# A two-layer block with routed experts on one Trainium2 core: empty slots left out of the row gather, and the gate matrix's last tile split like the others

## The chip, the cores and the metric

The program runs on one core of one Trainium2 chip. The metric is the device time of one execution in microseconds (us), lower is better. A core has four compute engines (TensorE or PE for matmuls, VectorE or DVE, ScalarE or ACT, GpSimd or POOL), an engine SyncE (SP) whose queue issues most of the DMAs, and 16 DMA engines that move data between the chip's memory (HBM) and the core's own memory. Each engine runs its instructions in order and waits for the others by semaphores.

## What is computed

The reference runs two blocks one after the other on 512 tokens of width 1024, each two layers deep. The first block is sparse attention beside a gated recurrence. The second block mixes (a short convolution in layer 0, a gated linear recurrence in layer 1), then sends each token through two of 32 experts. The part that the change touches is that expert step, which runs once in each layer of the second block:

```python
def hier_moe(x, w_rg, b_rg, w_re, b_re, w_gate, w_up, w_down):
    ...
    _, g_top = lax.top_k(pg, 1)             # one of 4 groups per token
    ...
    top_p, top_i = lax.top_k(pe, TOP_K)     # two of its 8 experts
    expert = g_top * EXPERTS_PER_GROUP + top_i
    weight = pg_top * top_p
    ...
    def expert_block(args):
        idx, e = args
        xb = x_pad[idx]                     # rows of the tokens sent to expert e
        hb = jax.nn.silu(xb @ w_gate[e]) * (xb @ w_up[e])
        return hb @ w_down[e]
    ...
    y = jnp.zeros((n + 1, d), x.dtype).at[tok_pad].add(contrib)
```

`w_gate` and `w_up` are 1024x512 per expert, `w_down` is 512x1024, all float32. 512 tokens times two choices make 1024 token-expert pairs per layer.

## The kernel before

**Precision by splitting.** A float32 weight tile is split into a high and a low part: ACT writes the high part (`wh`, line 425) and DVE the rest (`wl = w - wh`, line 426), both in a type that TensorE takes in one pass. The token rows are split alike. The 128 columns that TensorE holds still are 64 slots' high parts beside the same 64 slots' low parts, so two matmuls, one with `wh` and one with `wl`, give all four products. Both tensors come from rings: four tiles `wh`, four `wl`, and four tiles `X` that hold a high and a low part together (lines name `X<-w` and `X<-w,X`).

**Slots.** `route` (line 1336) ranks the tokens of each expert and fills 64 slots per expert. A matmul against one-hot rows gives, per slot and expert, one more than the number of the token-expert pair that sits there, or 0 for an empty slot. `tokens` (line 1483) makes the token number `tk` from it: less 1, not below 0, halved. An empty slot so names token 0. `slots` (line 1489) makes `mp`, the row to which the slot's result goes: less 1, plus 2^20 for an empty slot, which lies past the table's end. `rows` (line 1496) writes the normalised tokens to a table `xr` in HBM.

**Gather and scatter.** `gather` (line 1517) takes the rows of two experts (128 slots) from `xr` with one indirect DMA on POOL's queue (line 1522) into a tile `xg` from a ring of two, and then has PE transpose them, and ACT and DVE split them into `pk`, with the float32 copy of the last k-tile in `xf`. `finish` (line 1616) writes the 64 result rows of one expert with another indirect DMA (line 1624) to `ym` at the rows `mp`. Both are issued with a bound (`bounds_check`) beyond which a row is dropped without an error.

**The stream.** `experts` (line 1727) lists units of work. A weight tile `w` is 1 MB (128 partitions x 2048 float32), six per expert: two of gate (k = 0, 1), two of up (k = 2, 3), two of down (k = 4, 5), from a ring of six. SP issues their loads (line 1561), each once its buffer has been read. Each tile has two halves of 1024 columns, `part` 0 and 1; a half is one unit, except that k = 5 has one unit only. `cut` (line 1565) splits a unit's half into `wh`/`wl` or into `X`, and TensorE's matmuls for it come AHEAD = 6 units later in the program.

**The part left unsplit.** For three 512-column tiles per expert only the first 512 columns of the last half are split, and the other 512 (`also`) are multiplied in float32 with the unsplit rows:

```python
m = 1 if k in (1, 3) and part else 2
also = w[:, 3] if m == 1 else w[:, 2:4] if k == 5 else None
h, l = self.cut(w[:, 2 * part:2 * part + m], n // 4 % 2)
```

These are the last tile of gate (k = 1), of up (k = 3), and the last of down (k = 5). The float32 matmul stands at line 1583 (gate and up) and line 1612 (down). It reads the tile `w` itself, so that tile's buffer comes free only behind it.

**The order.** `pin` (line 1627) fixes each compute engine's order to the order in which the program lists its work. Per expert DVE's list has: the `wl` or `X` of eleven units, two adds for `yb` (line 1623) of the expert before, two multiplications for `mth` (lines 1597 and 1598), and the split `hk` (line 426) of the hidden rows. ACT has the high parts of the same, the copies of accumulators (lines 1765 and 1622), a tanh (line 1596), and `hk` (line 425), which needs `mth`. In every second expert, two `pk` splits and `xf` (line 1538) come in. TensorE's accumulators are three tiles `acc`; a new expert's first matmul waits until ACT has copied the up product out (line 1765).

A loop for experts with more than 64 tokens (line 1661) stands ahead of the stream; it runs zero times on this data. Its block `overflow` uses the same functions.

Of the kernel before, what the change touches and what calls it, by code (L numbers as in the profile page):

```python
# [13 lines left out]
I32 = mybir.dt.int32  # L14
# [3 lines left out]
OP = mybir.AluOpType  # L18
AX = mybir.AxisListType

P = 128
# [158 lines left out]
class Net:  # L180
# [1155 lines left out]
    def route(self, i):  # L1336
# [81 lines left out]
        for k in range(2):  # L1418
# [3 lines left out]
            for c in range(NC):  # L1422
                pe.matmul(mps, R[:, c].rearrange("p b s -> p (b s)"), idk[:, k, c], start=(k + c == 0),
                          stop=(k == 1 and c == NC - 1))
        tk = self.t([P, N_EXP // 2], "tk", 1, I32)
        tk2 = self.t([P, N_EXP], "tk2", 1, I32)
        self.tokens(tk2, mps)
        for b in range(2):
            v.tensor_copy(tk[b * BLK:(b + 1) * BLK], tk2[b * BLK:(b + 1) * BLK, b::2])
        mp = self.t([BLK, N_EXP], "mp", 1, I32)  # L1430
        self.slots(mp, mps[:BLK])

# [24 lines left out]
        def further():  # L1457
# [22 lines left out]
            return place, more  # L1480
        return table, tk, mp, further, weights

    def tokens(self, tk, ps):

        v = self.nc.vector
        v.tensor_scalar(tk, ps, -1.0, 0.0, op0=OP.add, op1=OP.max)
        v.tensor_scalar(tk, tk, 1, None, op0=OP.logical_shift_right)

    def slots(self, mp, ps):

        v = self.nc.vector
        em = self.t([BLK, N_EXP], "em", 1)[:, :ps.shape[1]]
        v.tensor_scalar(em, ps, 0.0, float(1 << 20), op0=OP.is_equal, op1=OP.mult)
        v.scalar_tensor_tensor(mp, ps, -1.0, em, op0=OP.add, op1=OP.add)
# [21 lines left out]

    def gather(self, table, idx, m):

        nc = self.nc
        v, act, pe = nc.vector, nc.scalar, nc.tensor  # L1520
        xg = self.t([P, D], "xg", 2)
        nc.gpsimd.indirect_dma_start(out=xg[:m], out_offset=None, in_=table[:, :],  # L1522
# [52 lines left out]

    def inner(self, ps, x, k, h, l, also):

        pe = self.nc.tensor
        pk, xf = x
        for q in range(h.shape[1]):  # L1580
            pe.matmul(ps, pk[:, k + q], h[:, q], start=(k + q == 0), stop=False)  # L1581
            if also is not None:
                pe.matmul(ps[0:BLK], xf, also, start=False, stop=False, skip_group_check=True)  # L1583
            pe.matmul(ps, pk[:, k + q], l[:, q], start=False, stop=also is not None)  # L1584

# [57 lines left out]
    def moe(self, i, xs, nxt):  # L1643
# [4 lines left out]
        table, tk, mp, further, weights = self.route(i)  # L1648
        pair = lambda q: self.gather(table, tk[:, q:q + 1], P)
        g = pair(0)  # L1650
# [10 lines left out]
        with self.tc.For_i(0, extra, 1) as b:  # L1661
# [14 lines left out]
            self.slots(mc, mps)  # L1676
            self.tokens(tc, mps)
            go = self.gather(table, tc, BLK)
            next(go)
# [20 lines left out]
    def overflow(self, i, e, x, mp, ym):  # L1700
# [3 lines left out]
        for up in range(2):  # L1704
            ps = self.acc()
            for k in range(0, KT, 2):
                w = self.weights(i, e, 2 * up + k // 4, k // 2 % 2)
                m = 1 if k == KT - 2 else 2
                h, l = self.cut(w[:, 0:m])
                self.inner(ps, x, k, h[:, :m], l[:, :m], w[:, 1] if m == 1 else None)  # L1710
            gu.append(room())
            self.nc.scalar.activation(gu[up], ps, AF.Copy)
# [14 lines left out]
    def experts(self, i, ws, xs2, pair, mp, ym, weights):  # L1727
# [14 lines left out]
        for n in range(len(units) + AHEAD):  # L1742
            if n < len(units):
                e, k, part = units[n]
                if part == 0 and (e, k) not in ws:
                    ws[e, k] = self.weights(i, e, k)
                w = ws[e, k]
                m = 1 if k in (1, 3) and part else 2
                also = w[:, 3] if m == 1 else w[:, 2:4] if k == 5 else None
                h, l = self.cut(w[:, 2 * part:2 * part + m], n // 4 % 2)  # L1750
                ready.append((h[:, :m], l[:, :m], also))
            self.pin()
# [205 lines left out]
```

## Time and profile before

| what | value |
|---|---|
| three timed runs | median 3081.84 us (3077.51 to 3083.08) |
| the profiled execution | 3084.05 us, of which the span of its instructions is 3082.3 us |
| busy share of the span | PE 93%, DVE 80%, ACT 57%, POOL 15% |
| mean granted TensorE clock | 0.975 of full speed |
| HBM traffic | 573.60 MB read, 31.49 MB written |

The profile is one execution of the same program. A busy share is an average over stages of different kinds; the two expert streams lie at about 1590 to 2130 us and 2445 to 2985 us of the span, and there the DMA engines are busy nearly all the time, elsewhere a fifth to a third.

### The profile page before, as it was taken

What the parts mean: (1) busy time and instruction counts of PE and PEld (TensorE: products, weight loads), DVE (VectorE), ACT (ScalarE), POOL (GpSimd) and SP (SyncE); (2) the same over time, 40 slices, a digit from 0 to 9 for tenths busy, and PEclk for the clock granted to TensorE, in tenths of its full rate; (3) what the DMA queues carried; (4) which work ended last, traced back from release to release, by engine and by line L of the source; (5) the groups of instructions that cost most, each with busy time, mean ns of one, the idle gap of its engine ahead of it and who ended that gap; (6) DMA issues with size and microseconds to landing.
All of it is one profiled execution on the core that took longest, in us unless ns stands there. A gap on an engine that the chain in (4) does not pass through costs nothing.

```text
span 3082.3 us, 39081 instructions
## 1 busy us (share of the span) xinstructions
PE 2881.6 (93%) x13517; PEld 2160.2 (70%) x13517; DVE 2464.3 (80%) x4540; ACT 1756.1 (57%) x2953; POOL 472.8 (15%) x457
## 2 busy tenths in 40 slices
PE   7998999999999999999979999998998799999987
PEld 6677778886787778878856666665776566666656
DVE  7899787867999578855558888887789588888876
ACT  3454343544454433542357877776476577777874
POOL 1111110011121010120011121111122111121112
PEclk9999999999999999999989999999999899999998
DMA  5211122242222222241259999997123399999981
GB/s 156 82 62 62 62 77 69 83 128 94 74 62 61 77 69 79 86 130 62 95 216 396 406 404 401 407 399 277 65 86 110 151 385 405 404 408 408 406 313 59
DMA packets 248663, 599.29 MB, mean 194 GB/s; under 512 B 29212, under 2 KB 159726, under 8 KB 215694
## 3 DMA queue, kind: packets, MB, share of 16 engines
q1 hardware_dynamic: 237582, 567.38, 49.1%
q0 software_dynamic: 10880, 29.37, 2.7%
q8 instruction: 108, 1.77, 0.2%
q14 instruction: 93, 0.76, 0.1%
HBM read 573.60 MB, written 31.49 MB: 196 GB/s over the span
## 4 chain that ended last, share of the span: by engine, by line
PE 38%; issue 33%; DVE 18%; POOL 7%; ACT 3%; DMA 2%; POOLq 0%; SPq 0%; ACTq 0%; DVEq 0%
PE acc L522 9%; PE acc L521 9%; PE acc L520 9%; POOL ym L1624 4%; DVE wl L426 3%; DVE tmp L953 2%; PE aux L432 1%; POOL xg L1522 1%; PE aux L463 1%; PE aux L843 1%; DMA xg<-xr,tk 1%; PE aux L1111 1%; PE aux L1106 1%; DVE r L1082 1%; DVE r L1081 1%
## 5 line engine op out<-in xcount | busy, mean ns | idle before, releaser
L425 ACT ACTIVATE wh<-w 128x1024 fp32r<-128x1024 f32 (+1 forms) x592 | 577.8, 1003 | 370.2 <-PE acc L521 323.0
L426 DVE TENSOR_TENSOR wl<-w,wh 128x1024 fp32r<-128x1024 f32 (+1 forms) x592 | 674.1, 1164 | 71.1 <-ACT wh L425 66.7
L520 PE MATMUL acc<-X,wh 128*128 128x512 f32 (+1 forms) x1504 | 606.3, 403 | 18.5 <-DVE tmp L898 6.4
L521 PE MATMUL acc<-X,wh 128*128 128x512 f32 (+1 forms) x1536 | 615.8, 401 | 0.6 <-DVE X L426 0.6
L522 PE MATMUL acc<-X,wl 128*128 128x512 f32 (+1 forms) x1504 | 601.9, 401 | 4.9 <-DVE wl L426 4.9
L426 DVE TENSOR_TENSOR X<-w,X 128x1024 fp32r<-128x1024 f32 (+1 forms) x352 | 380.9, 1122 | 64.0 <-ACT X L425 63.2
L425 ACT ACTIVATE X<-w 128x1024 fp32r<-128x1024 f32 (+1 forms) x352 | 326.7, 971 | 34.3 <-DMA w<-in_w_exp_gate_dram 10.1
L520 PEld LDWEIGHTS acc<-X,wh 128*128 128x128 f32 (+1 forms) x1504 | 285.3, 190 | 82.1 <-DVE tmp L898 7.3
L521 PEld LDWEIGHTS acc<-X,wh 128*128 128x128 f32 (+1 forms) x1536 | 291.3, 190 | 59.4 <-DVE X L426 1.2
L522 PEld LDWEIGHTS acc<-X,wl 128*128 128x128 f32 (+1 forms) x1504 | 284.8, 189 | 64.9 <-DVE wl L426 7.1
L1624 POOL DMA_INDIRECT ym<-yb,mp x64 | 136.0, 2125 | 811.9 <-DVE yb L1623 811.9
L1581 PE MATMUL acc<-X,pk 128*128 128x512 f32 x448 | 185.6, 414 | 18.2 <-ACT tmp L1765 12.6
L1581 PE MATMUL acc<-wh,pk 128*128 128x512 f32 x448 | 181.9, 406 | 15.5 <-ACT tmp L1765 15.5
L1584 PE MATMUL acc<-X,pk 128*128 128x512 f32 x448 | 185.9, 415 | 0.0
L1584 PE MATMUL acc<-wl,pk 128*128 128x512 f32 x448 | 183.5, 410 | 0.0
L1583 PE MATMUL acc<-w,xf 128*64 128x512 f32 x256 | 137.3, 618 | 0.0
L1584 PEld LDWEIGHTS acc<-X,pk 128*128 128x128 f32 x448 | 86.3, 193 | 66.0 <-DVE X L426 18.7
L1593 PEld LDWEIGHTS aux<-fold,tmp 128*128 128x128 f32 x1024 | 126.1, 194 | 8.8 <-ACT tmp L1765 3.5
L1584 PEld LDWEIGHTS acc<-wl,pk 128*128 128x128 f32 x448 | 84.5, 189 | 65.8 <-issue 16.2
L479 POOL TENSOR_TENSOR tmp<-tmp,tmp 128x512 f32<-128x512 f32 x60 | 86.4, 1444 | 280.9 <-ACT tmp L472 234.5
L1593 PE MATMUL aux<-fold,tmp 128*128 128x64 f32 x1024 | 123.2, 274 | 3.2 <-ACT tmp L1765 3.2
L1612 PE MATMUL acc<-w,mth 128*64 128x512 f32 x256 | 123.6, 605 | 0.0
(564 smaller groups left out, 5331.8 us busy)
## 6 DMA issues: line engine op xcount, KB each, us to landing
w<-in_w_exp_gate_dram SPq DMA_DIRECT2D x128, 1024.0 KB, 8.0
w<-in_w_exp_up_dram SPq DMA_DIRECT2D x128, 1024.0 KB, 7.8
w<-in_w_exp_down_dram SPq DMA_DIRECT2D x128, 1024.0 KB, 8.4
w<-in_w_in_dram SPq DMA_DIRECT2D x72, 1024.0 KB, 5.1
w<-in_w_in_a_dram SPq DMA_DIRECT2D x12, 1024.0 KB, 5.0
w<-in_w_out_dram SPq DMA_DIRECT2D x8, 1024.0 KB, 5.0
w<-in_w_ple_gate_dram SPq DMA_DIRECT2D x8, 1024.0 KB, 12.1
X<-ym SPq DMA_DIRECT2D x16, 512.0 KB, 5.4
```

The costliest lines, as they stand in the source:

```text
L425: self.nc.scalar.activation(h, x, AF.Copy)
L426: self.nc.vector.tensor_sub(l, x, h.bitcast(F32))
L479: nc.gpsimd.tensor_add(t, tot[0], sq)
L520: mm(ps, wh[:, k], xh[k], start=(k == 0), stop=False)
L521: mm(ps, wh[:, k], xl[k], start=False, stop=False)
L522: mm(ps, wl[:, k], xh[k], start=False, stop=(k == kt - 1))
L1581: pe.matmul(ps, pk[:, k + q], h[:, q], start=(k + q == 0), stop=False)
L1583: pe.matmul(ps[0:BLK], xf, also, start=False, stop=False, skip_group_check=True)
L1584: pe.matmul(ps, pk[:, k + q], l[:, q], start=False, stop=also is not None)
L1593: pe.matmul(fp[:, (4 * q + f) * BLK:(4 * q + f + 1) * BLK], gu[q][:, f * P:(f + 1) * P], self.fold, start=True, stop=True)
L1612: pe.matmul(pss[c][0:BLK], hv[:, 3], also[:, c], start=False, stop=False, skip_group_check=True)
L1624: return nc.gpsimd.indirect_dma_start(out=ym[:, :], out_offset=bass.IndirectOffsetOnAxis(ap=mp, axis=0), in_=y, in_offset=None, bounds_che ...
```

## The change

`mp` is now made first, for all 128 partitions, and `tk` is `mp` halved. An empty slot so names row 524287 of a table of 512 rows, and the gather's bound leaves that row out: nothing is written to its row of `xg`, which keeps what was there. So that this is a number, the two `xg` tiles are taken once per layer, set to zero by POOL, and used in turn by the gathers.

Beside it the gate's last tile (k = 1) has its last 512 columns split too (m = 2), so its float32 matmul goes; up (k = 3) and down (k = 5) keep theirs. `inner` gets a flag that says which unit is a product's last, since the float32 term no longer tells.

```diff
@@ -1423,12 +1423,12 @@
         tk = self.t([P, N_EXP // 2], "tk", 1, I32)
+        mp = self.t([P, N_EXP], "mp", 1, I32)
         tk2 = self.t([P, N_EXP], "tk2", 1, I32)
-        self.tokens(tk2, mps)
+        self.slots(mp, mps)
+        self.tokens(tk2, mp)
...
-        mp = self.t([BLK, N_EXP], "mp", 1, I32)
-        self.slots(mp, mps[:BLK])
...
-    def tokens(self, tk, ps):
+    def tokens(self, tk, mp):
+
+        self.nc.vector.tensor_scalar(tk, mp, 1, None, op0=OP.logical_shift_right)
...
-        v.tensor_scalar(tk, ps, -1.0, 0.0, op0=OP.add, op1=OP.max)
-        v.tensor_scalar(tk, tk, 1, None, op0=OP.logical_shift_right)
...
-    def gather(self, table, idx, m):
+    def gather(self, table, idx, m, xg):
...
-        xg = self.t([P, D], "xg", 2)
...
-    def inner(self, ps, x, k, h, l, also):
+    def inner(self, ps, x, k, h, l, also, last):
...
-            pe.matmul(ps, pk[:, k + q], l[:, q], start=False, stop=also is not None)
+            pe.matmul(ps, pk[:, k + q], l[:, q], start=False, stop=last and q == n - 1)
...
-        pair = lambda q: self.gather(table, tk[:, q:q + 1], P)
+        xg = [self.t([P, D], "xg", 2) for _ in range(2)]
+        for x in xg:
+            nc.gpsimd.memset(x, 0.0)
+        pair = lambda q: self.gather(table, tk[:, q:q + 1], P, xg[q % 2])
...
-                m = 1 if k in (1, 3) and part else 2
+                m = 1 if k == 3 and part else 2
                 also = w[:, 3] if m == 1 else w[:, 2:4] if k == 5 else None
                 h, l = self.cut(w[:, 2 * part:2 * part + m], n // 4 % 2)
-                ready.append((h[:, :m], l[:, :m], also))
+                ready.append((h[:, :m], l[:, :m], also, k in (1, 3) and part == 1) if k < 4 else (h, l, also))
```

What moves is seen in the order of instructions. On DVE, this is the second expert pair of the first layer's stream, from the split of the gathered rows (`pk`) to the second half of the next up tile; before:

```order
L426 TENSOR_TENSOR pk_14919<-aux_14921,pk_14919 128x8x64
L426 TENSOR_TENSOR pk_14919<-aux_14928,pk_14919 128x8x64
L426 TENSOR_TENSOR wl_14937<-w_14910,wh_14936 128x1024
L426 TENSOR_TENSOR wl_14947<-w_14944,wh_14946 128x1024
L426 TENSOR_TENSOR wl_14956<-w_14944,wh_14955 128x512
L426 TENSOR_TENSOR wl_14968<-w_14965,wh_14967 128x1024
L426 TENSOR_TENSOR X_14975<-w_14965,X_14975 128x1024
L1623 TENSOR_TENSOR yb_14984<-acc_14959,tmp_14985 64x512
L1623 TENSOR_TENSOR yb_14984<-acc_14960,tmp_14988 64x512
L426 TENSOR_TENSOR X_14996<-w_14994,X_14996 128x1024
L426 TENSOR_TENSOR X_15008<-w_14994,X_15008 128x512
```

and in the change:

```order
L426 TENSOR_TENSOR pk_14920<-aux_14922,pk_14920 128x8x64
L426 TENSOR_TENSOR pk_14920<-aux_14929,pk_14920 128x8x64
L426 TENSOR_TENSOR wl_14938<-w_14911,wh_14937 128x1024
L426 TENSOR_TENSOR wl_14948<-w_14945,wh_14947 128x1024
L426 TENSOR_TENSOR wl_14957<-w_14945,wh_14956 128x1024
L426 TENSOR_TENSOR wl_14969<-w_14966,wh_14968 128x1024
L426 TENSOR_TENSOR X_14976<-w_14966,X_14976 128x1024
L1621 TENSOR_TENSOR yb_14985<-acc_14960,tmp_14986 64x512
L1621 TENSOR_TENSOR yb_14985<-acc_14961,tmp_14989 64x512
L426 TENSOR_TENSOR X_14997<-w_14995,X_14997 128x1024
L426 TENSOR_TENSOR X_15008<-w_14995,X_15008 128x512
```

The third `wl` behind `pk` has 1024 columns in place of 512; nothing else in DVE's order moves, and so for each of the 64 experts (32 in either layer). ACT's order differs in the same place alone: the `wh` that goes with it has 1024 columns.

On PE this is the end of the same expert's gate product; before, with the float32 matmul of 64 columns held still (`xf`) between the high and the low one:

```order
L1581 MATMUL acc_15003<-wh_14946,pk_14919 128x512
L1584 MATMUL acc_15003<-wl_14947,pk_14919 128x512
L1581 MATMUL acc_15003<-wh_14955,pk_14919 128x512
L1583 MATMUL acc_15003<-w_14944,xf_14920 64x512
L1584 MATMUL acc_15003<-wl_14956,pk_14919 128x512
L1581 MATMUL acc_15055<-wh_14967,pk_14919 128x512
```

and in the change:

```order
L1579 MATMUL acc_15003<-wh_14947,pk_14920 128x512
L1582 MATMUL acc_15003<-wl_14948,pk_14920 128x512
L1579 MATMUL acc_15003<-wh_14956,pk_14920 128x512
L1582 MATMUL acc_15003<-wl_14957,pk_14920 128x512
L1579 MATMUL acc_15003<-wh_14956,pk_14920 128x512
L1582 MATMUL acc_15003<-wl_14957,pk_14920 128x512
L1579 MATMUL acc_15056<-wh_14968,pk_14920 128x512
```

One float32 matmul is gone and two of the one-pass kind have come.

On POOL this is the issue of the last two table writes and of the first gather in a layer; before:

```order
L1507 DMA xr_14322<-xg_14351 128x1024
L1507 DMA xr_14322<-xg_14365 128x1024
L1522 DMA xg_14468<-xr_14322,tk_14458 128x1024
```

and in the change:

```order
L1505 DMA xr_14322<-xg_14351 128x1024
L1505 DMA xr_14322<-xg_14365 128x1024
L1649 MEMSET xg_14467 128x1024
L1649 MEMSET xg_14468 128x1024
L1519 DMA xg_14467<-xr_14322,tk_14458 128x1024
```

Two fills of 128x1024 stand ahead of the first gather in either layer. The rest of POOL's order and SP's order of loads are as before.

## Rows read from the trace of the kernel before

**Rows 1.** Both streams: engines' busy time in each stretch, clock, DMA share, GB/s.

```profile
1609.00:2108.00 499.00, 483.71 (x2046) 309.59 (x2045) 441.69 (x524) 394.33 (x560) 85.00 (x43) 1.00 1.00 402
2468.00:2966.00 498.00, 485.19 (x2044) 311.79 (x2043) 441.26 (x523) 393.35 (x558) 82.76 (x43) 0.99 1.00 402
```

**Rows 2.** What PE waited for in the first stream.

```profile
PE acc L1581 <- ACT tmp L1765: 15.3, 17, 1.9
```

**Rows 3.** What ACT waited for in the first stream: us, times, longest.

```profile
ACT hk L425 <- DVE mth L1598: 70.7, 31, 2.6
...
ACT X L425 <- DMA w<-in_w_exp_gate_dram: 2.5, 4, 1.0
...
ACT X L425 <- DMA w<-in_w_exp_up_dram: 1.6, 3, 1.1
ACT wh L425 <- DMA w<-in_w_exp_gate_dram: 1.2, 2, 0.8
ACT wh L425 <- DMA w<-in_w_exp_up_dram: 1.1, 4, 0.4
```

**Rows 4.** DVE's groups of instructions by form in the first stream.

```profile
L426 DVE TENSOR_TENSOR X<-w,X 128x1024 fp32r<-128x1024 f32 x136 | 161.8, 1220 | 20.9 <-ACT X L425 20.4
...
L426 DVE TENSOR_TENSOR X<-w,X 128x512 fp32r<-128x512 f32 x30 | 20.4, 680 | 0.0
...
L426 DVE TENSOR_TENSOR hk<-mth,hk 128x256 fp32r<-128x256 f32 x30 | 12.8, 425 | 14.5 <-ACT hk L425 14.5
```

**Rows 5.** DVE in order of time: start, duration, idle before; the split hk alone.

```profile
1645.51 0.42 DVE L426 TENSOR_TENSOR hk<-mth,hk 128x256 fp32r<-128x256 f32 x1 [0.48 <-ACT hk L425]
...
1810.70 0.43 DVE L426 TENSOR_TENSOR hk<-mth,hk 128x256 fp32r<-128x256 f32 x1 [0.49 <-ACT hk L425]
...
1828.32 0.43 DVE L426 TENSOR_TENSOR hk<-mth,hk 128x256 fp32r<-128x256 f32 x1 [0.48 <-ACT hk L425]
...
1843.35 0.43 DVE L426 TENSOR_TENSOR hk<-mth,hk 128x256 fp32r<-128x256 f32 x1 [0.48 <-ACT hk L425]
...
2108.12 0.43 DVE L426 TENSOR_TENSOR hk<-mth,hk 128x256 fp32r<-128x256 f32 x1 [0.48 <-ACT hk L425]
...
2503.39 0.43 DVE L426 TENSOR_TENSOR hk<-mth,hk 128x256 fp32r<-128x256 f32 x1 [0.48 <-ACT hk L425]
...
2966.14 0.42 DVE L426 TENSOR_TENSOR hk<-mth,hk 128x256 fp32r<-128x256 f32 x1 [0.48 <-ACT hk L425]
```

**Rows 6.** The page: POOL's DMA queue: packets, MB, share of 16 engines.

```profile
q0 software_dynamic: 10880, 29.37, 2.7%
```

**Rows 7.** DMAs issued by POOL: size of each, median us to landing.

```profile
xr<-xg POOLq DMA_DIRECT2D x8, 512.0 KB, 2.9
...
xg<-xr,tk POOLq DMA_INDIRECT x32, 9.3
```

**Rows 8.** ACT's groups of instructions by form in the same stretch.

```profile
L425 ACT ACTIVATE X<-w 128x1024 fp32r<-128x1024 f32 x137 | 138.8, 1048 | 4.3 <-DMA w<-in_w_exp_gate_dram 2.5 <-DMA w<-in_w_exp_up_dram 1.6
...
L425 ACT ACTIVATE X<-w 128x512 fp32r<-128x512 f32 x30 | 18.7, 624 | 0.0
```

**Rows 9.** PE in order of time, around one float32 matmul of a gate.

```profile
1824.76 0.40 PE L1584 MATMUL acc<-X,pk 128*128 128x512 f32 x1
1825.00 0.40 PE L1581 MATMUL acc<-X,pk 128*128 128x512 f32 x1
1825.33 1.07 PE L1583 MATMUL acc<-w,xf 128*64 128x512 f32 x2
...
1826.67 0.39 PE L1581 MATMUL acc<-X,pk 128*128 128x512 f32 x1
```

**Rows 10.** POOL's largest fill in the trace.

```profile
L1073 POOL MEMSET ty<- 128x512 f32 x16 | 7.9, 524 | 0.0
```

**Rows 11.** PE after its longest wait in the second stream.

```profile
2495.22 0.50 PE L1581 MATMUL acc<-wh,pk 128*128 128x512 f32 x1 [1.99 <-ACT tmp L1765]
```

**Rows 12.** A stretch soon behind that wait, columns as in Rows 1.

```profile
2497.00:2503.00 6.00, 6.00 (x24) 5.21 (x22) 5.87 (x8) 3.57 (x7) 2.24 (x1) 0.50 1.01 393
```

More of the change, by code (lines that the diff above doesn't have):

```diff
@@ L1480, in further @@
             return place, more
-        return table, tk, mp, further, weights
-    def tokens(self, tk, ps):
-        v = self.nc.vector
-        v.tensor_scalar(tk, ps, -1.0, 0.0, op0=OP.add, op1=OP.max)
-        v.tensor_scalar(tk, tk, 1, None, op0=OP.logical_shift_right)
+        return table, tk, mp[:BLK], further, weights
+    def tokens(self, tk, mp):
+        self.nc.vector.tensor_scalar(tk, mp, 1, None, op0=OP.logical_shift_right)
     def slots(self, mp, ps):
         v = self.nc.vector
-        em = self.t([BLK, N_EXP], "em", 1)[:, :ps.shape[1]]
+        em = self.t([P, N_EXP], "em", 1)[:ps.shape[0], :ps.shape[1]]
         v.tensor_scalar(em, ps, 0.0, float(1 << 20), op0=OP.is_equal, op1=OP.mult)
@@ L1574, in cut @@
         return h, l
-    def inner(self, ps, x, k, h, l, also):
+    def inner(self, ps, x, k, h, l, also, last):
         pe = self.nc.tensor
         pk, xf = x
-        for q in range(h.shape[1]):
+        n = h.shape[1]
+        for q in range(n):
             pe.matmul(ps, pk[:, k + q], h[:, q], start=(k + q == 0), stop=False)
@@ L1676, in moe @@
             self.slots(mc, mps)
-            self.tokens(tc, mps)
-            go = self.gather(table, tc, BLK)
+            self.tokens(tc, mc)
+            go = self.gather(table, tc, BLK, xg[1])
             next(go)
@@ L1709, in overflow @@
                 h, l = self.cut(w[:, 0:m])
-                self.inner(ps, x, k, h[:, :m], l[:, :m], w[:, 1] if m == 1 else None)
+                self.inner(ps, x, k, h[:, :m], l[:, :m], w[:, 1] if m == 1 else None, k == KT - 2)
             gu.append(room())
```

## The prediction

> **What bounds the kernel now.** I read the two expert streams alone, since nothing else changes. The busy times of both stretches come first [rows 1]: the DMA engines are 100% busy at 402 GB/s, PE 97% (483.71 of 499 us), DVE 89%, ACT 79%. By this table the transfers are the limit, then PE, and the change would relieve both. A share does not say who waits for whom, so the waits come next. PE waited 15.3 us in the first stream, always for ACT's copy of an accumulator [rows 2]. ACT waited 70.7 us for DVE's `mth`, some 2.3 us in each expert, and only 6.4 us (2.5 + 1.6 + 1.2 + 1.1) for weights to land [rows 3]. DVE's idle time in front of its splits and of `hk` is put down to ACT [rows 4]. So ACT and DVE wait for each other, hardly for a landing, and PE waits for them.
>
> The order of time settles it. From one `hk` split on DVE to the next is one expert. The expert with the gathered rows' split takes 17.62 us (1810.70 to 1828.32), the one without it 15.03 us (1828.32 to 1843.35), together 32.65 us for a pair [rows 5]. The 28 experts from 1645.51 to 2108.12 take 462.61 us, where 14 such pairs would take 457.1: 5.5 us over. The 28 from 2503.39 to 2966.14 take 462.75 us, 5.7 us over. That excess is about what ACT waited for landings (6.4 us). I conclude that the list of work of DVE, with its hand-overs to ACT, sets the pace at 32.65 us a pair, and that late weights add 0.4 us to reach 33.04. DMA and PE run at nearly the same pace, but they follow.
>
> **The change, part by part.**
>
> *Fewer rows gathered.* POOL's queue moved 29.37 MB [rows 6]. The eight table writes are 8 x 0.524 = 4.19 MB [rows 7]; the 32 gathers [rows 7] of 128 rows of 4 KB are 16.78 MB; what is left, 8.40 MB, is the scatter: 2050 rows of 4 KB, where 64 scatters of 64 slots name 4096. Half the slots are empty, and the scatter's bound leaves their rows out today. The gather will leave out the same 2048 rows, 8.39 MB. A pair moves 402 GB/s x 33.04 us = 13.28 MB now; less 64 rows of 4 KB it is 13.02 MB, 32.4 us at the same rate. Nothing in DVE's, ACT's or PE's lists gets shorter. What this part can give back in the streams is the time for which landings are late: between 0 and 11.2 us (5.5 + 5.7). I take all 11.2, because the transfers will need 32.4 us of a pair that takes longer than before (below).
>
> The Trainium skill speaks for this part and against my reading: Perfetto Trace Analysis, section Identifying the Most-Contended Engine, takes the engine with the highest occupancy, for DMA the HBM utilization, as the bottleneck to be worked on first, and its section on the roofline gives 358 GB/s as a core's peak, with some 120% as what one core alone reaches. The 402 GB/s are 112% of that, against 89% for DVE; by that rule the streams would shorten with the bytes, which is the first rival below. The waits on landings, 6.4 us in 499, do not agree with it.
>
> *The gate's last 512 columns split.* In each of 64 experts one DVE instruction goes from 512 to 1024 columns. The means are 680 and 1220 ns [rows 4]: 0.54 us more. Its ACT partner goes from 624 to 1048 ns [rows 8]: 0.42 us more. ACT has 2.3 us of waiting for DVE behind it in every expert [rows 3], so ACT's part is hidden; if that cover were gone, 0.42 x 64 = 27 us would lie on the path in its place. DVE's part has no cover: between the gate's split and `hk` DVE works through its list without a wait in the 17.62 and 15.03 us above, and ACT's wait for `mth` grows by it. So 64 x 0.54 = 34.6 us on the path, bounded below by 0 if DVE's idle time could take it up. I take all of it, since that idle time (0.48 us ahead of `hk` [rows 5], the rest ahead of splits whose high part ACT has just begun) is the hand-over itself and comes whatever stands before it. A pair then takes 32.65 + 1.08 = 33.73 us.
>
> *PE.* From 1825.00 to 1826.67 one high, one float32 and one low matmul take 1.67 us; a plain matmul starts every 0.24 us (1824.76 to 1825.00) [rows 9]. Four of them take 0.96 us, so PE saves 0.7 us in an expert, 45 us in all. None of that is on the path: PE waits already, 1.0 us in a pair (15.3 us in 15 pairs) [rows 2], and will wait about 1.0 + 1.4 + 0.7 = 3.1 us. The gate's tile `w` is now freed by DVE's split and not by the float32 matmul behind it, so its next load starts earlier; that helps the landings counted above.
>
> *POOL.* Two fills of 128x1024 in each layer, in front of the first gather. The trace has 524 ns for 128x512 [rows 10], so about 1.05 us each, 4.2 us in all. The first tile is free before the last table write lands, so its fill is hidden; the second has to wait for that landing, and the gather for it. Against that, the gathers of the opening, when the weights are still on their way, bring 0.26 MB less each, 0.65 us at 402 GB/s. I put the openings at 0, between +4 and -4 us. DVE's chain to `tk` has one small instruction more, which goes under in these bounds.
>
> **Sum,** against the profiled execution's own 3084.05 us: 3084.05 + 34.6 - 11.2 = 3107.4 us. That execution lies 2.2 us above the median of the three timed runs, so 3105 us is the forecast for the median, 0.75% slower.
>
> **The rivals.**
>
> *The DMA engines are the bound, and it gets faster.* For it speaks their 100% share [rows 1]; against it that ACT hardly waits for a landing and that so many experts take 15.03 or 17.62 us, whatever the transfers do. Then 8.39 MB / 402 GB/s = 20.9 us go, and the profiled time would be 3063 us, the median 3061. It decides if DVE, with 33.73 us a pair, could be pushed below 32.4; I see no way. Chance 0.09.
>
> *DVE's idle time takes up the longer split.* DVE is idle in 11% of the stream. Then only the late landings go: 3084 - 11.2 - 2.2 = 3070.6. The instants above speak against it. Chance 0.05. If it takes up half, + 17.3 - 11.2 gives 3088, no change that can be told. Chance 0.06.
>
> *PE's clock falls.* After PE had waited 1.99 us at 2495.22 [rows 11], the granted clock was 0.50 from 2497 to 2503 [rows 12], that is 1.2 in place of 2.4 GHz, and PE lost 3 us in those 6. Waits of up to 1.9 us in the first stream [rows 2] left it at 1.00 [rows 1]. With 3.1 us to wait in a pair, most of it in one place (the new accumulator in the expert with the gather), the clock may fall in many pairs. PE's spare 3.1 us would then be used up, its `fold` matmuls and the release of buffers would come late, and ACT has 2.3 us to absorb that. If 0.7 us of the 3 comes through in each of 32 pairs, it costs 22 us: 3127. At worst all 3 us come through in each second pair, 48 us. Chance 0.10. In small doses it belongs to my main case.
>
> *The change doesn't do what it says,* and rows are still fetched. The scatter's bytes speak against it. It would cost at most the 11.2 us again, 3116, less what the longer pair gives the landings anyhow; I count it in the main case.
>
> **How the numbers follow.** The main case, DVE's list plus 1.08 us a pair, has 0.70 and its own range from 3093 (a third of the longer split hidden) to 3120 (no landing gained, 4 us at the openings). The DMA rival and the idle rival stand at 3061 and 3071. Changes under 0.2%, 6 us, can't be told from none in this kernel. Faster: 0.09 + 0.05 = 0.14. Same: 0.06. Slower: 0.80. The range 3085 to 3128 holds the main case, the half-hidden one and the clock's middle price; it leaves out the two fast cases and the clock's worst, under 0.2 in all.
>
> **What would show it.** In the profile after, the `hk` splits on DVE should stand 18.16 and 15.57 us apart. ACT's wait for `mth` should be 2.4 us an expert, its wait for landings near 0, DMA's share in the streams some 96%, and POOL's queue should have moved 21 MB. PE's wait for ACT's copy should be about 3 us a pair, and PE's busy time in the streams fall. I am wrong if the distance of the `hk` splits shrinks to some 16.2 us on average with ACT waiting for landings (the DMA was the bound), or if it grows beyond 16.9 on average with ACT waiting for PE (the clock).

## The result and the profile after

The changed kernel takes 3102.36 us (median of 6 runs, 3099.03 to 3103.71) against 3082.46 us (3077.51 to 3085.08): ratio 1.0063, 95% interval 1.0053 to 1.0073. It is slower by 0.63%, 2.6 us under the forecast. The profiled execution took 3099.03 us, the fastest of the six; its span is 3097.2 us. Line numbers differ between the kernels by up to three.

POOL's queue on the page after, against [rows 6]:

```profile
q0 software_dynamic: 10880, 20.99, 1.9%
```

The rows of empty slots are gone, 29.37 - 20.99 = 8.38 MB, in as many packets as before. Busy time in both streams, columns as in [rows 1] (PE, PE's weight loads, DVE, ACT, POOL, each with its count of instructions, then granted clock, DMA share and GB/s); each stretch is 30 experts, as there:

```profile
1609.00:2118.00 509.00, 472.32 (x2045) 323.62 (x2045) 457.11 (x523) 403.96 (x557) 72.08 (x43) 0.98 0.98 387
2473.00:2983.00 510.00, 476.13 (x2050) 327.01 (x2048) 457.54 (x523) 404.75 (x560) 72.09 (x43) 0.97 0.98 388
```

From the first `hk` split to the last but one the streams take 510.0 us each, 11.4 and 11.7 us more than before (498.6 and 498.3). DMA is no longer at 1.00, PE is busy 11 and 9 us less, DVE 15 and 16 us more. What ACT and PE waited for in the first stream (us, times, longest), against [rows 3] and [rows 2]:

```profile
ACT hk L425 <- DVE mth L1596: 71.1, 29, 2.7
ACT xf L1535 <- DVE pk L426: 25.4, 15, 1.7
...
ACT mth L1594 <- PE aux L1591: 1.8, 2, 1.1
```

```profile
PE acc L1579 <- ACT tmp L1766: 30.4, 15, 2.5
PE acc L1607 <- ACT tmp L1766: 6.2, 10, 0.6
```

No landing stands among ACT's waits any more, in the second stream neither. PE waits 36.6 us in 15 pairs, 2.4 us a pair, where it was 1.0. ACT's wait at `xf`, 1.7 us a pair, is part of a hand-over that comes up again below. DVE in order of time around three `hk` splits (start, duration, idle before and its releaser):

```profile
1814.40 0.42 DVE L426 TENSOR_TENSOR hk<-mth,hk 128x256 fp32r<-128x256 f32 x1 [0.48 <-ACT hk L425]
1815.35 4.74 DVE L426 TENSOR_TENSOR wl<-w,wh 128x1024 fp32r<-128x1024 f32 x4 [0.53 <-ACT wh L425]
1820.00 1.28 DVE L426 TENSOR_TENSOR pk<-aux,pk 128x512 fp32r<-128x512 f32 x2
1822.57 4.75 DVE L426 TENSOR_TENSOR X<-w,X 128x1024 fp32r<-128x1024 f32 x4 [1.29 <-ACT X L425]
...
1832.65 0.43 DVE L426 TENSOR_TENSOR hk<-mth,hk 128x256 fp32r<-128x256 f32 x1 [0.48 <-ACT hk L425]
...
1848.21 0.43 DVE L426 TENSOR_TENSOR hk<-mth,hk 128x256 fp32r<-128x256 f32 x1 [0.48 <-ACT hk L425]
```

The distances are 18.25 and 15.56 us, 33.81 a pair, where [rows 5] have 17.62 and 15.03. Before, the same two waits stand in the expert that begins at 1810.70 [rows 5]:

```profile
1811.64 4.74 DVE L426 TENSOR_TENSOR wl<-w,wh 128x1024 fp32r<-128x1024 f32 x4 [0.52 <-ACT wh L425]
...
1818.87 4.12 DVE L426 TENSOR_TENSOR X<-w,X 128x1024 fp32r<-128x1024 f32 x4 [1.29 <-ACT X L425]
```

So the waits on the list stayed as they were, 0.48 and 0.53 us at each `hk` and 1.29 us behind the gathered rows' split; the list itself got longer.

### The profile page after: what moved, and what is told of

It is laid out like the page before. It is cut to its first block, busy times and chain, and to the rows that moved or that the text cites. A ratio compares the mean times of both kernels' runs of the same rounds, so it can differ in the third digit from the quotient of the medians.

```text
span 3097.2 us, 39081 instructions
## 1 busy us (share of the span) xinstructions
PE 2860.0 (92%) x13517; PEld 2191.4 (71%) x13517; DVE 2498.5 (81%) x4538; ACT 1779.8 (57%) x2953; POOL 452.1 (15%) x461
## 2 busy tenths in 40 slices
DMA packets 248663, 590.91 MB, mean 191 GB/s; under 512 B 31260, under 2 KB 161774, under 8 KB 215694
## 3 DMA queue, kind: packets, MB, share of 16 engines
q0 software_dynamic: 10880, 20.99, 1.9%
q8 instruction: 108, 1.77, 0.2%
## 5 line engine op out<-in xcount | busy, mean ns | idle before, releaser
L425 ACT ACTIVATE wh<-w 128x1024 fp32r<-128x1024 f32 (+1 forms) x592 | 590.5, 1026 | 362.9 <-PE acc L521 325.1
L426 DVE TENSOR_TENSOR wl<-w,wh 128x1024 fp32r<-128x1024 f32 (+1 forms) x592 | 692.1, 1194 | 63.5 <-ACT wh L425 59.1
L426 DVE TENSOR_TENSOR X<-w,X 128x1024 fp32r<-128x1024 f32 (+1 forms) x352 | 397.6, 1170 | 55.7 <-ACT X L425 54.9
L425 ACT ACTIVATE X<-w 128x1024 fp32r<-128x1024 f32 (+1 forms) x352 | 339.2, 1009 | 23.1 <-issue 9.6
L1622 POOL DMA_INDIRECT ym<-yb,mp x64 | 118.7, 1854 | 884.0 <-DVE yb L1621 884.0
L1579 PE MATMUL acc<-X,pk 128*128 128x512 f32 x480 | 202.0, 421 | 37.5 <-ACT tmp L1766 29.7
L1579 PE MATMUL acc<-wh,pk 128*128 128x512 f32 x480 | 197.2, 411 | 29.7 <-ACT tmp L1766 29.7
L1582 PE MATMUL acc<-X,pk 128*128 128x512 f32 x480 | 199.1, 415 | 0.0
L1582 PE MATMUL acc<-wl,pk 128*128 128x512 f32 x480 | 195.4, 407 | 0.0
L1579 PEld LDWEIGHTS acc<-X,pk 128*128 128x128 f32 x480 | 94.3, 196 | 64.3 <-ACT tmp L1766 36.7
L1579 PEld LDWEIGHTS acc<-wh,pk 128*128 128x128 f32 x480 | 92.2, 192 | 55.0 <-ACT tmp L1766 36.6
L1582 PEld LDWEIGHTS acc<-X,pk 128*128 128x128 f32 x480 | 94.8, 198 | 43.8 <-DVE hk L426 8.9
```

Source lines behind the costliest of these rows:

```text
L425: self.nc.scalar.activation(h, x, AF.Copy)
L426: self.nc.vector.tensor_sub(l, x, h.bitcast(F32))
L1582: pe.matmul(ps, pk[:, k + q], l[:, q], start=False, stop=last and q == n - 1)
L1622: return nc.gpsimd.indirect_dma_start(out=ym[:, :], out_offset=bass.IndirectOffsetOnAxis(ap=mp, axis=0), in_=y, in_offset=None, bounds_che ...
```

## The experiments

The kernels ran in four sets, each beside the kernel before on one chip. Before measured 3082.4 us in the set of gather_only, split_only, split_both and yb_pool, 3083.3 in that of no_gate_f32, short_whole and short_split, 3081.5 in that of hk_split, xf_split, short_before and short_split_only, and 3081.4 beside short_split_no_f32.

### Each part alone

**gather_only**: the new gather, the gate's last tile unsplit as before.

```diff
-                m = 1 if k == 3 and part else 2
+                m = 1 if k in (1, 3) and part else 2
```

> The gather leaves out the empty slots' rows; the gate's last tile is treated as before. Theory (DVE's list with its hand-overs to ACT sets the pace): a pair of experts takes the 32.65 us of an undisturbed pair, the waits on landings (11.2 us in both streams) go and nothing else, so about 3071 us, 0.35% faster, with ACT's wait for landings near 0. Rival (the transfers set the pace): 8.39 MB at 402 GB/s go, 20.9 us, 3061 us. Second rival (landings cost nothing, the gain in the changed kernel came from elsewhere): 3082 us.

Measured 3074.04 us, ratio 0.9975 [0.9966, 0.9984]: faster by 8 us, nearer to the theory (3071) than to no change. **split_only**: the kernel before with the gate split, all rows gathered (the same line of the list of units, the other way, with the flag that `inner` needs for it).

```diff
-                m = 1 if k in (1, 3) and part else 2
+                m = 1 if k == 3 and part else 2
```

> The gate's last 512 columns are split, the gather fetches all rows. Theory: DVE's list takes 33.8 us a pair as in the changed kernel, the transfers need 33.3 us of it, so few landings are late: 3102 to 3107 us. Rival (the smaller gather was what took the late landings away): they stay, 11 us more than the changed kernel, 3113 us. Rival (transfers set the pace): no slower than before, 3082 us.

Measured 3109.05 us, ratio 1.0084 [1.0071, 1.0098], 2 us above the range that I gave. The two parts add up: -8.4 + 26.7 = +18.3 us, and the change has +19.9. DVE in order of time, `hk` alone, first with the gather alone and then with the split alone:

```profile
1873.79 0.42 DVE L426 TENSOR_TENSOR hk<-mth,hk 128x256 fp32r<-128x256 f32 x1 [0.48 <-ACT hk L425]
...
1891.41 0.42 DVE L426 TENSOR_TENSOR hk<-mth,hk 128x256 fp32r<-128x256 f32 x1 [0.48 <-ACT hk L425]
...
1906.79 0.43 DVE L426 TENSOR_TENSOR hk<-mth,hk 128x256 fp32r<-128x256 f32 x1 [0.48 <-ACT hk L425]
```

```profile
1819.89 0.42 DVE L426 TENSOR_TENSOR hk<-mth,hk 128x256 fp32r<-128x256 f32 x1 [0.49 <-ACT hk L425]
...
1838.14 0.43 DVE L426 TENSOR_TENSOR hk<-mth,hk 128x256 fp32r<-128x256 f32 x1 [0.48 <-ACT hk L425]
...
1853.71 0.43 DVE L426 TENSOR_TENSOR hk<-mth,hk 128x256 fp32r<-128x256 f32 x1 [0.48 <-ACT hk L425]
```

The split alone gives the 18.25 and 15.57 of the change. The gather alone leaves 17.62, and 15.38 in an expert where a weight landed late (15.03 in others). Over 28 experts of the first stream a pair took 33.04 us before, 32.82 with the gather alone (late landings went from 0.4 to 0.2 us, not to 0), 33.81 with the split alone, 33.80 with both. So in the streams of the changed kernel the new gather gives nothing: the longer list alone already has the weights in time.

### The split made twice

**split_both**: up's last tile split as well; no float32 matmul is left in gate and up.

```diff
-                m = 1 if k == 3 and part else 2
+                m = 2
```

> As the changed kernel, and up's last 512 columns are split too, so a second DVE instruction per expert goes from 512 to 1024 columns and a second float32 matmul goes. Theory: another 0.54 us an expert on DVE, 64 x 0.54 = 35 us, 3137 us, hk splits 16.1 and 18.8 us apart, though PE loses another 0.7 us of work per expert. Rival (PE or the transfers set the pace): at most the 3102 us of the changed kernel.

Measured 3137.74 us, ratio 1.0180 [1.0166, 1.0194]; 35.4 us above the changed kernel, where 64 x 0.54 is 34.6. DVE in order of time, `hk` alone:

```profile
1703.99 0.42 DVE L426 TENSOR_TENSOR hk<-mth,hk 128x256 fp32r<-128x256 f32 x1 [0.48 <-ACT hk L425]
...
1720.08 0.42 DVE L426 TENSOR_TENSOR hk<-mth,hk 128x256 fp32r<-128x256 f32 x1 [0.48 <-ACT hk L425]
...
1738.87 0.43 DVE L426 TENSOR_TENSOR hk<-mth,hk 128x256 fp32r<-128x256 f32 x1 [0.49 <-ACT hk L425]
```

The distances are 16.09 and 18.79 us, as expected, a pair takes 34.88. PE lost as many float32 matmuls again, and it bought nothing.

### TensorE relieved, VectorE not

**no_gate_f32**: as gather_only, without the gate's float32 matmuls, so that one term of the gate is missing.

```diff
-                also = w[:, 3] if m == 1 else w[:, 2:4] if k == 5 else None
+                also = w[:, 3] if m == 1 and k == 3 else w[:, 2:4] if k == 5 else None
```

> The kernel with the new gather and the old, unsplit last tile of each gate half, but the two float32 matmuls of that tile (0.5 us each on TensorE) are left out: one term of the gate is missing, and TensorE has about 1 us an expert less to do while VectorE's and ScalarE's lists are those of the run with the new gather alone (3074 us). Theory (VectorE's list and its hand-overs set the pace, TensorE is off the path): the same 3074, within 3070 to 3077, the pair of experts still 32.65 us. Rival (TensorE, busy 484 of 495 us in a stream, is what bounds): up to 1 us an expert less, 64 of them, so 3010 to 3030, or 3062 where the weights' transfers stop it first.

Measured 3067.6 us, ratio 0.9952 [0.9938, 0.9965]: 6.5 us under gather_only, 2.4 below the theory's range, far from the rival's 3010 to 3030. The first stream (columns as in [rows 1]):

```profile
1612.00:2105.00 493.00, 463.04 (x1992) 316.68 (x1991) 440.78 (x523) 392.15 (x559) 84.77 (x43) 0.97 0.99 400
```

PE has 21 us less to do than with the gather alone (484.35 of 495), and from the first `hk` to the last but one the streams are 2.2 and 2.8 us shorter, those of the landings: in the first stream ACT waited 0.2 us for weights in place of 3.4, and the average pair is 32.67 us. The end of each stream is 1 us shorter as well (see the tails below). That the buffers come free earlier, without the float32 matmul that read them last, fits the landings and was not tested by itself. PE was no bound in the streams.

### Work moved off VectorE's list, the wrong way

**yb_pool**: the changed kernel, with the addition of the two result halves moved from DVE to POOL, and ACT copying the other half out of the accumulator for it.

```diff
-            nc.vector.tensor_add(y[:, half * S:(half + 1) * S], ps[0:BLK], yl)
+            yh = y[:, half * S:(half + 1) * S]
+            nc.scalar.activation(yh, ps[0:BLK], AF.Copy)
+            nc.gpsimd.tensor_add(yh, yh, yl)
```

> As the changed kernel, but the two yb adds per expert leave DVE: ACT copies the low half of the accumulator too, and POOL adds the two. DVE's list gets 1.2 us shorter per expert, ACT's 1.0 us longer, which its 2.4 us of waiting for mth covers. Theory: DVE's list falls from 33.8 to 31.4 us a pair, below what the transfers need (32.4), so the transfers set the pace: (33.8 - 32.5) x 32 = 42 us less than the changed kernel, about 3060 us, and ACT waits for landings again. Rival (POOL's reads of SBUF slow DVE's two-input splits): the splits get longer than 1220 ns and part or all of it is lost, up to 3102 us. Rival (ACT becomes the bound): 3102 us or more with no wait of ACT for mth.

Measured 3180.34 us, ratio 1.0323 [1.0309, 1.0337], 120 us above what I expected. DVE, ACT and POOL in order of time, a fence each:

```profile
1772.04 1.22 DVE L426 TENSOR_TENSOR X<-w,X 128x1024 fp32r<-128x1024 f32 x1
1775.06 2.28 DVE L426 TENSOR_TENSOR X<-w,X 128x1024 fp32r<-128x1024 f32 x2 [1.80 <-ACT X L425]
```

```profile
1771.64 0.60 ACT L1620 ACTIVATE tmp<-acc 64x512 f32<-64x512 f32 x1
1772.27 0.59 ACT L1622 ACTIVATE yb<-acc 64x512 f32<-64x512 f32 x1
1772.88 0.59 ACT L1620 ACTIVATE tmp<-acc 64x512 f32<-64x512 f32 x1
1773.48 0.59 ACT L1622 ACTIVATE yb<-acc 64x512 f32<-64x512 f32 x1
1773.98 1.57 ACT L425 ACTIVATE X<-w 128x1024 fp32r<-128x1024 f32 x2
```

```profile
1772.94 2.71 POOL L1623 TENSOR_TENSOR yb<-yb,tmp 64x512 f32<-64x512 f32 x2 [13.51 <-ACT yb L1622]
```

ACT now makes four copies in a row, from 1771.64 to 1774.07, before it writes the next high part, and DVE, which has taken up what ACT had made before, stands 1.80 us (1.53 in the expert without a gather). That is more than the two additions of 0.67 us that left the list. The rest is a price on DVE's own splits: of 300 splits of 128x1024 in a stream the 240 that ran beside no addition of POOL took 1.22 us, the 60 beside one took 1.52 on average and up to 1.99 (half of them kept their 1.22). A pair went to 36.16 us. POOL's two additions took 2.71 us here, and the split from 1775.06 lay beside the second. ACT's spare time is at `mth`, 2.4 us an expert, and does nothing for copies that stand in another place. The list is not DVE's alone: where DVE takes up a fresh high part, ACT's order counts.

### The hand-overs taken off the list

If the list with its waits sets the pace, then the waits themselves can go. Two edits, both on the changed kernel. In **hk_split** DVE rounds the high half of `hk` itself, so that neither waits for the other there:

```diff
-        self.split(hk[:, :, 0:BLK], hk[:, :, BLK:P], hv)
+        v.tensor_copy(hk[:, :, 0:BLK], hv)
+        v.tensor_sub(hk[:, :, BLK:P], hv, hk[:, :, 0:BLK].bitcast(F32))
```

In **xf_split** ACT copies `xf` ahead of the last split of the gathered rows, and so no longer stands behind DVE's low part:

```diff
-            self.split(o[:, :, :, 0:BLK], o[:, :, :, BLK:P], tv)
             if half:
                 act.activation(xf, tv[:, 3], AF.Copy)
+            self.split(o[:, :, :, 0:BLK], o[:, :, :, BLK:P], tv)
```

> The changed kernel with hk's high half rounded on VectorE (0.29 us by short_split's row) and xf left where it was. Each expert loses the waits of 0.48 and 0.53 us and pays 0.29: 0.72 less, a pair 33.81 to 32.37. Theory (list and hand-overs): 3102 less 64 times 0.72 = 3056, within 3050 to 3064. Rival (the waits move to another place, since ScalarE must still deliver): above 3085.

> The changed kernel with xf copied ahead of pk's last split, and hk left as it was. Each pair loses the wait of 1.29 us: 33.81 to 32.52. Theory: 3102 less 32 times 1.29 = 3061, within 3056 to 3068; the wait for hk (0.48 and 0.53) stays. With hk_split the two add up to more than the 75 us that both gave together, because TensorE and landings stop it there. Rival (the wait moves): above 3085.

Measured 3054.6 us, ratio 0.9914 [0.9901, 0.9928], and 3056.74 us, ratio 0.9919 [0.9905, 0.9932]: each turns the slower change into a faster kernel. DVE in order of time, `hk` alone, of hk_split and then of xf_split:

```profile
1709.08 0.42 DVE L1600 TENSOR_TENSOR hk<-mth,hk 128x256 fp32r<-128x256 f32 x1
...
1726.48 0.43 DVE L1600 TENSOR_TENSOR hk<-mth,hk 128x256 fp32r<-128x256 f32 x1
...
1741.20 0.42 DVE L1600 TENSOR_TENSOR hk<-mth,hk 128x256 fp32r<-128x256 f32 x1
```

```profile
1711.56 0.42 DVE L426 TENSOR_TENSOR hk<-mth,hk 128x256 fp32r<-128x256 f32 x1 [0.48 <-ACT hk L425]
...
1728.31 0.43 DVE L426 TENSOR_TENSOR hk<-mth,hk 128x256 fp32r<-128x256 f32 x1 [0.48 <-ACT hk L425]
...
1743.87 0.42 DVE L426 TENSOR_TENSOR hk<-mth,hk 128x256 fp32r<-128x256 f32 x1 [0.48 <-ACT hk L425]
```

17.40 and 14.72 us with the one, 16.75 and 15.56 with the other, for 18.25 and 15.56 before the edits. That is 0.85 us at each `hk` and 1.50 a pair at `xf`, more than the 0.72 and 1.29 that I expected. Part of the rest is in the starts of single splits: in a row they start 1.14 us apart, and in the changed kernel the third one behind each of these waits started 1.24 us after the second, which went with the wait. No wait came back in another place of DVE's list.

Both edits together were run on all four combinations of the change's parts: **short_before** (neither part), **short_whole** (the new gather), **short_split_only** (the split), **short_split** (both).

> The kernel before (gather of all rows, unsplit last tile) with only the two hand-overs taken off VectorE's list, neither part of the change. With the new gather the same edit gave 3043.7 us, TensorE 100% busy there. Theory (TensorE bounds it too, the bigger gather costs what it cost on the full list or a little more as the weights come close): 3044 to 3058. Rival (the weights and the gather together are now the floor, 8.4 MB at 411 GB/s are 20 us): 3060 to 3066.

> New gather, unsplit last tile, and two hand-overs to ScalarE taken off VectorE's list: VectorE rounds hk's high half itself (an estimate from the 0.42 us row of the low half: 0.2 to 0.4 us) in place of waiting 0.48 us for ScalarE and then 0.53 us for its next split; and ScalarE copies xf ahead of pk's last split, so that the 1.29 us wait of each pair goes. By VectorE's list alone a pair would fall from 32.65 to about 30 us. TensorE's busy time, 484 us of a stream, is 32.3 a pair, and the weights at the 402 GB/s that the streams of before reached are 489 us, 32.6 a pair. Theory: VectorE stops being what bounds, and the others take over at once: 3058 to 3068, little under the 3074 of the new gather alone, with TensorE waiting for landings or nothing. Rival (a busy DMA share is no floor, and TensorE is no bound): 2990 to 3010.

> The split alone (gather of all rows) with the two hand-overs off VectorE's list; with the new gather this gave 3027.3 us, VectorE and TensorE 98% busy and DMA at 419 GB/s. Theory (the split pays once TensorE and not VectorE's list bounds; the gather's bytes add waits for landings): 3030 to 3045, and less than short_before by 10 to 18 us. Rival (the split paid there only because the gather's bytes were gone): no less than short_before.

> The changed kernel (gather and split as in the change) with the same two hand-overs taken off VectorE's list. Its pair of experts took 33.81 us; without the 1.29 us wait and with some 0.76 us less at each hk it would be 31.0 by VectorE's list, TensorE's 472 us of a stream are 31.5 a pair, the weights at 402 GB/s 32.6. Theory (list paces, and the weights' transfers are the floor just behind it): 3055 to 3068, ScalarE waits for landings again and the split costs nothing any more against its twin without it. Rival 1 (DMA is no floor): 3020 to 3035. Rival 2 (the pace is not VectorE's list with its hand-overs but its work or something else): within 3090 to 3104, no gain.

Medians in us, with the ratio to before and its interval for the new ones:

```
                    list as it was      hand-overs off the list
neither part        3082.4              short_before      3051.82  0.9901 [0.9886, 0.9916]
new gather          3074.04             short_whole       3043.69  0.9869 [0.9853, 0.9885]
split               3109.05             short_split_only  3044.76  0.9871 [0.9855, 0.9888]
both (the change)   3102.36             short_split       3027.34  0.9814 [0.9798, 0.9831]
```

On the list as it was the split costs 27 to 28 us with either gather. With the hand-overs gone the same split gives back 7 us with the old gather and 16 with the new. The first streams of short_before, short_whole, short_split_only and short_split, one fence each, columns as in [rows 1]:

```profile
1615.00:2050.00 435.00, 434.41 (x1846) 280.41 (x1847) 405.08 (x503) 355.27 (x479) 77.05 (x40) 1.00 1.01 417
```

```profile
1615.00:2050.00 435.00, 434.86 (x1853) 281.29 (x1850) 405.97 (x504) 354.84 (x479) 80.55 (x40) 1.00 1.01 411
```

```profile
1615.00:2050.00 435.00, 424.38 (x1844) 283.87 (x1843) 417.46 (x501) 363.62 (x479) 68.48 (x39) 1.00 1.01 418
```

```profile
1615.00:2050.00 435.00, 429.44 (x1893) 290.92 (x1892) 425.88 (x512) 372.30 (x490) 70.78 (x40) 1.00 1.01 419
```

An average pair takes 31.89, 31.92, 31.86 and 31.18 us in this order, and from the first `hk` to the last but one the two streams together take 960.6, 959.6, 961.3 and 943.1 us. So neither part alone shortens the streams, and both together shorten them by 17 us. Without the split PE is busy all 435 us, and the smaller gather gives nothing there: TensorE is the bound. With the split and the old gather PE has 11 us free, and taking the 0.26 MB of empty slots out of a pair gives 0.68 us, where 0.26 MB at 418 GB/s are 0.63: there the transfers hold it. The 7 us that the split gives with the old gather are therefore not in the streams; 3 of them stand in the tails (13.03 and 12.12 us in short_before, 11.09 and 11.06 in short_split_only; more on the tails below). Two of my expectations failed on one number: for short_whole and short_split I had taken 402 GB/s as the most that the transfers give, and the kernels ran faster than that floor allows, at 411 and 419 GB/s, so that short_split fell into its first rival's range. For short_split_only I expected 10 to 18 us less than short_before and got 7. short_before came as expected.

**short_split_no_f32**: short_split without up's float32 matmuls, so that one term of up is missing.

```diff
-                also = w[:, 3] if m == 1 else w[:, 2:4] if k == 5 else None
+                also = w[:, 2:4] if k == 5 else None
```

> The fastest kernel so far (change plus short list, 3027.3 us, pair 31.18 us on average) with the two float32 matmuls of the up matrix's last tile left out, so that one term of up is missing. TensorE has 1 us an expert, 2 us a pair, less to do (it was busy 429 of 435 us, 30.8 a pair, and would have 28.8); VectorE's and ScalarE's lists are the same, 30.4 us a pair by VectorE's work; the bytes are the same. Four kernels whose bytes differ have come to rest between 411 and 419 GB/s; 13.02 MB a pair at 418 GB/s are 31.15 us. Theory (now the transfers are the floor, at 418 and not at the 402 GB/s that I had taken): the pair stays at 31.0 to 31.2, 3021 to 3029 us, GB/s no higher than 420. Rival (TensorE is still the bound): a pair falls to VectorE's 30.4 to 30.6, 3002 to 3012 us, at 425 to 428 GB/s.

Measured 3023.28 us, ratio 0.9813 [0.9800, 0.9827]. The same stretch:

```profile
1615.00:2050.00 435.00, 411.39 (x1838) 283.32 (x1837) 424.95 (x512) 370.92 (x489) 70.21 (x40) 1.00 1.01 419
```

PE has 18 us less to do, and an average pair takes 31.23 us, as before this edit. TensorE is not what holds short_split. The rate is again 419 GB/s, and ACT's largest waits in that stretch are for landings:

```profile
ACT wh L425 <- DMA w<-in_w_exp_gate_dram: 23.5, 19, 1.6
ACT X L425 <- DMA w<-in_w_exp_gate_dram: 20.6, 17, 2.1
```

Little of this reaches DVE, which is busy 425 of the 435 us and waited 6 us for ACT's high parts. In short_split a pair that no late landing disturbs takes 15.92 + 14.72 = 30.64 us:

```profile
1644.63 0.43 DVE L1600 TENSOR_TENSOR hk<-mth,hk 128x256 fp32r<-128x256 f32 x1
...
1660.55 0.43 DVE L1600 TENSOR_TENSOR hk<-mth,hk 128x256 fp32r<-128x256 f32 x1
...
1675.27 0.42 DVE L1600 TENSOR_TENSOR hk<-mth,hk 128x256 fp32r<-128x256 f32 x1
```

The average of 31.18 us is 0.54 more. So DVE's list and the transfers now stand within 2% of each other; no run takes bytes away from short_split, so which of them holds it is open.

## Why the prediction was right, point by point

**What bounds.** The list of DVE with its hand-overs set the pace, as predicted. The list made longer by one split costs 64 x 0.54 (change, split_both), PE relieved without touching the list changes only late landings and the tails (no_gate_f32), and waits taken off the list shorten it by their length and a little more (hk_split, xf_split). The most contended engine by its share, the DMA rival and the rule of the Trainium skill that spoke for it (Perfetto Trace Analysis, section Identifying the Most-Contended Engine), did not name the bound: taking 8.38 MB away gave 8 us, not 21. With the hand-overs gone the bytes do count: they hold short_split_only, and 0.54 us of a pair in short_split is late landings.

**The gate's last columns split: +34.6 us predicted.** The expert without a gather grew by 0.53 us (predicted 0.54), the one with it by 0.63. The pair grew by 1.16 us in place of 1.08, which is +37 us in 32 pairs. The odd 0.1 us comes from ACT's longer half, which I had put down as hidden. The high and the low part of the gate's last columns in the expert with the gather, before and then in the change:

```profile
1820.16 0.63 ACT L425 ACTIVATE X<-w 128x512 fp32r<-128x512 f32 x1
1821.15 0.69 DVE L426 TENSOR_TENSOR X<-w,X 128x512 fp32r<-128x512 f32 x1
```

```profile
1823.87 1.06 ACT L425 ACTIVATE X<-w 128x1024 fp32r<-128x1024 f32 x1
1824.96 1.23 DVE L426 TENSOR_TENSOR X<-w,X 128x1024 fp32r<-128x1024 f32 x1
```

Before, ACT had ended at 1820.79, 0.36 us ahead of DVE's start. In the change it ends at 1824.93, and DVE starts 1.24 us after its last split in place of 1.14, in each of the 15 pairs of the first stream. The cover was looked for at the wrong place: ACT's wait at `mth`, still 2.4 to 2.7 us, stands behind this split. In the other expert ACT's longer half stayed hidden.

**Fewer rows gathered: -11.2 us predicted, from late landings.** The landings are on time, but split_only shows that the longer list does this with the old gather too; the prediction touched on that only under its last rival. What the gather brought, 6.7 us between split_only and the change, stands mostly in the openings, which I had put at 0 within 4 us. From DVE's first instruction on the slots' numbers (`mp` in the change, `tk` before) to the first `hk` the change takes 32.7 and 32.6 us in the two layers (1575.97 to 1608.63, 2440.51 to 2473.12), split_only 34.4 and 36.2, before 34.2 and 36.1. The two openings together take 69.5 to 70.6 us in the four profiles with the old gather and 64.1 to 66.7 in the ten with the new one: some 5 us. The fills, 0.95 us each where I had 1.05, held nothing up: the first gather follows that first instruction after 3.8 and 4.5 us, where before it took 3.8 and 5.2, and the second gather follows the first after 6.0 and 5.1 us in place of 6.8 and 6.5. gather_only gained in the same two places, 6 us in the streams and 6 in the openings of its profile, so its median of 8 us less is not the landings alone.

A mis-sized term and a misplaced one, then, whose sum came out near; that the forecast lay within 3 us is in part luck. The streams grew by 11.36 + 11.68 = 23.0 us (60 of the 64 experts) where the terms give 34.6 - 11.2 = 23.4, and the profiled execution's span grew by 14.9: 5.0 us went in the openings, 2.0 in the tails and 1.1 in stretches that the change does not touch. The medians grew by 19.9, since the profiled execution after is the fastest of its six.

**The tails.** From the last `hk` but one to the last, before takes 12.56 us, the change 11.56, split_only 11.55 and gather_only 12.52. no_gate_f32, which only leaves the gate's float32 matmuls out, takes 11.53 there. So at the end of a stream the gate's float32 matmul is on the path, and the split gains 1 us a layer; splitting up's as well (split_both, 11.54) gives no more. I had not counted it.

**PE's clock.** It fell, as the rival said, and cost nothing, as the main case said. The changed kernel between two `hk` splits 18.24 us apart, 1645.38 and 1663.62 (columns as in [rows 1]):

```profile
1645.00:1655.00 10.00, 7.64 (x26) 3.58 (x24) 7.85 (x9) 8.29 (x13) 1.02 (x1) 1.00 0.96 349
1655.00:1665.00 10.00, 9.99 (x38) 8.67 (x39) 8.93 (x12) 7.55 (x11) 1.64 (x1) 0.66 1.00 400
```

PE was idle 2.4 of 10 us, and in the next 10 the granted clock was 0.66, part of the time at 1.2 GHz. `fold`, the matmuls ahead of the tanh, came late, ACT waited 0.65 and 1.14 us for it in this expert and the next, and its wait for `mth` shrank by as much (1.77 and 1.56 in place of 2.4 and 2.66). The granted clock was 0.50 in twelve places of the two streams, 48 us in all, where before it was so in one, for 7 us. The `hk` splits kept their distance: from the fourth of a stream to the last but one, each stands 18.24 to 18.26 or 15.55 to 15.56 us after the one before it. The cover held.

The clock also took half of what PE was to save. I had 0.7 us an expert, 21 us in 30 experts, and PE is busy only 11 and 9 us less. The clock of 0.98 and 0.97 over the streams makes up for the rest, by my estimate (2% of 509 us and 3% of 510 are 10 and 15 us). PE's waits came to 2.4 us a pair where I had 3.1.

## What to carry to other kernels

When two engines hand work to and fro in a fixed order, time the distance between two recurrences of one instruction and add up its list with the waits in it: that sum, not the largest busy share, told what an edit would cost here. A trade of one engine's time for another's pays only where the relieved engine is the bound; here the same split, with the new gather, cost 28 us with the hand-overs in the list and gave 16 us once two of them, worth 0.85 us at each `hk` and 1.50 us a pair, had been taken out by two small edits. So before a part of a change is dropped as slower, look for waits on the same list that can be removed, and measure the part again beside them.

## What the runs showed of the hardware

**A share of 1.00 was not the most that the transfers give.** The DMA engines showed a share of 1.00 at 402 GB/s before [rows 1], and the short lists ran at 411 to 419 GB/s with a share of 1.01. Three kernels whose bytes or PE work differ rest at 418, 419 and 419. The Trainium skill (Perfetto Trace Analysis, section on the roofline) gives 358 GB/s with some 120% as a lone core's practical ceiling, by my estimate 430 GB/s. The rate of 419 GB/s is 117%, which agrees; no run here shows where the ceiling lies.

**Dropped rows leave their packets.** POOL's queue has 10880 packets before and after, for 29.37 and 20.99 MB; the packets under 512 B on the page went from 29212 to 31260, by the 2048 empty slots.

**An addition on POOL slows a split on DVE.** In yb_pool a split that lay beside POOL's addition for 0.90 us took 1.98 us in place of 1.22, and one begun 0.63 us ahead of an addition kept its 1.22 while the addition took 1.75 in place of 1.31. The Trainium skill (SBUF — State Buffer, section Who interferes with whom) says that a DVE instruction with two inputs in SBUF and a GpSimd instruction that reads SBUF exclude each other for a whole instruction, and the one that comes second waits. The durations agree in direction and nearly in size: the split took 0.76 us longer for 0.90 us beside the addition, the addition 0.44 us longer for 0.59 beside the split.
